# A hybrid-mixer trunk on one core: the GLA decay beside its values, the mLSTM weight products among the pairs

## Chip, core and metric

One of the eight cores of a Trainium2 chip runs the whole kernel. The metric is the device time of one execution in microseconds (us), taken as the median of several. The core has a matrix engine (PE, TensorE), a vector engine (DVE), a scalar engine (ACT), GpSimd (POOL), SyncE (SP, which here only issues transfers) and 16 DMA engines.

## What is computed

For 2048 tokens of width 1024 the reference computes one layer: RMSNorm, a combined input projection, four causal token mixers in parallel (a gated linear recurrence RG-LRU, an mLSTM with matrix memory, an HGRN2 recurrence and a gated linear attention, GLA), a projection of each mixer's output, a merge by sigmoid gates, an output projection, the residual and a final RMSNorm. All is float32.

```python
u = jnp.einsum('bsd,de->bse', h, w_in).astype(jnp.float32)
...
q = headwise(xm, m_wq)
k = headwise(xm, m_wk)
v = headwise(m_x, m_wv)
qkv = jnp.concatenate([q, k, v], axis=-1)
log_i = qkv @ m_wi + m_bi
log_f = jax.nn.log_sigmoid(qkv @ m_wf + m_bf)
...
log_gk = jax.nn.log_sigmoid(g_lr @ g_w_lr2 + g_b_lr2) / GLA_GATE_TAU
og = gla_chunkwise(split_heads(g_q, GLA_HEADS), split_heads(g_k, GLA_HEADS),
                   split_heads(g_v, GLA_HEADS), split_heads(log_gk, GLA_HEADS))
...
proj = jnp.einsum('bsnw,nwd->bsnd', branches, w_branch)
gates = jax.nn.sigmoid(merge.reshape(B, S, N_BRANCH, D_MODEL))
merged = jnp.sum(gates * proj, axis=2)
return merged @ w_out
```

The change touches the two places where small weights meet: the products of mLSTM's q, k and v weights with each other and with the gate weights (they need no token), and GLA's decay `log_gk`, a product of rank 16.

## The kernel before

The tokens go through in two halves of 1024. Products are in float32 split into a high and a low part (tiles hh and hl of the activations, wh and wl of the weights), three matmuls for each. Each half has these stages, with the times of the first half:

- A prologue, 0 to about 100 us, once: `load_first` loads and scales tokens and computes the first gates (`proj_ch`, L268), `load_h` the other 512 tokens (L685 spreads the norm factors over the partitions with four small products into one bank, ACT copies them at L686, and eight L688 on DVE scale the tokens), `setup_mix` prepares constants, and `split_blocks` forms block sums (L375 to L378) and their splits (L305, L306).
- The pairs, to about 740 us: `ahead_pairs` computes two output tiles at a time by seven products of half size (`ip_pair`, L423, with sums L428 of weights and L432 of results on DVE). The order of the pairs and of the steps between them is the table GORD. Projected rows go to DRAM.
- The mixers, to about 1200 us: `mixers` runs twelve steps of HGRN and GLA tiles (`gla_tile`, L959 to L1107; its scans are L968 and L970, its last products L1102 and sums L1103), and the generator `mlstm` beside them. Direct projections fill PE meanwhile: `ip_vals` (L280, its results copied at L1123 and, for the 8 columns of the low-rank decay in each of two groups, to lrt at L1125) and the gates of `gates_ahead`.
- The merge, to about 1290 us: four branches, each with its input read back and split (`branch`, L1292 and L1293), then products L268 with the gate applied at L1319; and `outp`.

What sets the order on the engines is a scheduler that simulates a timeline; instructions are emitted under `prio` offsets (EV 6000 for loads and evacuations, MIX 4000 for mixers), and the scheduler takes ready ones by priority. Buffers then decide who waits: the arena is a list of slots of 516 columns, given out in turn (`T` one slot, `F` two), so whoever writes a slot waits for the last reader of its earlier contents. PSUM has eight banks: two of them (pb, by `pbank`) take the direct projections in turn, six (mx, by `bank`) the mixers and small products. In the pairs all eight go round.

`setup_rows` does not exist before. Its work stands in `setup_mix`, L612 to L634: five loads (mwv, three weights of 512 columns and m_wg of 96), two memsets, and for each of four heads four products (L623 of 128x128; L626, L627 and L631 of 8 columns) in three banks, with five DVE copies (L624 to mqk, L628 and L629 to gx, L632 and L633 to gv).

`gla_decay` turns lrt round (eight transposes L1168, two copies L1169 into the slot pair lt), multiplies it by wlr (four products L1175) and puts each through ACT (L1177 to L1179 and a logarithm) and DVE (L1181, L1182). The mixers call it ahead of step 7; its results are used from step 8 on, while `ip_vals(3)`, which completes lrt, is called ahead of step 6.

Of the kernel before, what the change touches and what calls it, by code (L numbers as in the profile page):

```python
# [38 lines left out]
SI = 6  # L39
RLAT = 2000  # L40
LAT = -600
GORD = [('g',2),('r',1),('z',1),('g',1),('z',1),('r',1),('g',1),('z',2),('r',1),('g',1),('z',2),('r',1),('z',6),('g',3),('t',0),('m',0),('g',1),('m',0),('g',1),('m',0),('g',1),('m',0),('d',0),('m',0),('g',99),('d',1),('z',2)]
NORM = {"hz": "hnw", "gz": "gnw"}
SILU = ("lz", "mz", "hq", "hz", "gz")
FILL = [0, 2, 0, 0, 0, 1, 0, 0, 1, 0, 0, 0, 2, 0]
# [102 lines left out]
class Trunk:  # L148
# [312 lines left out]
        fin(c)  # L461
        self.free(*c)

    def ahead_pairs(self):


        nc = self.nc
# [70 lines left out]
        first = True  # L538
        for n, i in GORD:
            if n == "t":  # L540
                self.exp_ln()
            elif n == "m":
                with self.prio(RLAT):
                    next(rows, None)
            if n in "tm":
                continue
            for tiles, fin in ({"g": g, "z": z, "r": r}[n][:i] if n != "d" else [decays([2 * i, 2 * i + 1])]):
                self.ip_pair(*tiles, fin, first)
                first = False
            if n != "d":  # L550
                del {"g": g, "z": z, "r": r}[n][:i]
# [39 lines left out]
    def setup_mix(self):  # L591
        nc, c, a, col = self.nc, self.const, self.a, self.col
        V, A = nc.vector, nc.scalar

        lam = self.pvt[:, PV["lam"][0]:PV["lam"][0] + 4]
        t = col(4)
        self.clru = col(4)
        A.activation(t, lam, AF.Abs)
        A.activation(t, t, AF.Exp, scale=-1.0)
        A.activation(t, t, AF.Ln, bias=1.0)  # L600
        V.tensor_scalar(self.clru, lam, -1.0, 0.0, op0=ALU.mult, op1=ALU.max)
        V.tensor_tensor(self.clru, self.clru, t, op=ALU.add)
        V.tensor_scalar(self.clru, self.clru, 4.0, None, op0=ALU.mult)
        self.nclru = col(4)
        V.tensor_scalar(self.nclru, self.clru, -1.0, None, op0=ALU.mult)
        self.hba, self.hbx = col(4), col(4)
        V.tensor_scalar(self.hba, self.pvt[:, PV["ba"][0]:PV["ba"][0] + 4], 0.5, None, op0=ALU.mult)
        V.tensor_scalar(self.hbx, self.pvt[:, PV["bx"][0]:PV["bx"][0] + 4], 0.5, None, op0=ALU.mult)

        o = PV["mcw"][0]  # L610
        V.tensor_scalar(self.hmc, self.pvt[:, o:o + 20], 0.5, None, op0=ALU.mult)
        nc.sync.dma_start(self.mwv, a["m_wv"])  # L612
        V.memset(self.gx, 0.0)
        V.memset(self.gv, 0.0)
        wt = [self.T() for _ in range(3)]
        for w, n in zip(wt, ("m_wqT", "m_wkT", "m_wvT")):
            nc.sync.dma_start(w[:, :512], a[n].rearrange("p h d -> p (h d)"))
        wg = self.T()
        nc.sync.dma_start(wg[:, :96], a["m_wg"])
        for h in range(4):  # L620
            ps = self.bank()
            wq, wk, wv = (w[:, h * 128:(h + 1) * 128] for w in wt)
            nc.tensor.matmul(ps[:, 0:128], wq, wk, start=True, stop=True)  # L623
            V.tensor_copy(self.mqk[:, h], ps[:, 0:128])  # L624
            ps = self.bank()
            nc.tensor.matmul(ps[:, 0:8], wq, wg[:, h * 8:h * 8 + 8], start=True, stop=False)  # L626
            nc.tensor.matmul(ps[:, 0:8], wk, wg[:, 32 + h * 8:40 + h * 8], start=False, stop=True)  # L627
            V.tensor_copy(self.gx[:, h, 0:4], ps[:, 0:4])  # L628
            V.tensor_copy(self.gx[:, h, 32:36], ps[:, 4:8])  # L629
            ps = self.bank()  # L630
            nc.tensor.matmul(ps[:, 0:8], wv, wg[:, 64 + h * 8:72 + h * 8], start=True, stop=True)  # L631
            V.tensor_copy(self.gv[:, h, 0:4], ps[:, 0:4])  # L632
            V.tensor_copy(self.gv[:, h, 32:36], ps[:, 4:8])  # L633
        self.free(*wt, wg)  # L634

        lbl = self.pvt[:, PV["lbl"][0]:PV["lbl"][0] + 4]
        e, r, self.l1, self.alb, z = col(4), col(4), col(4), col(4), col(4)
        V.tensor_tensor(e, lbl, lbl, op=ALU.subtract)
        A.activation(e, e, AF.Exp)
        V.reciprocal(r, e)  # L640
        V.tensor_tensor(e, e, r, op=ALU.mult)
        V.tensor_tensor(e, e, e, op=ALU.subtract)
        A.activation(self.l1, e, AF.Ln, scale=-1.0, bias=1.0)
        V.tensor_scalar(z, e, 0.0, -1e30, op0=ALU.is_le, op1=ALU.mult)
        V.tensor_scalar(r, e, 1e-37, None, op0=ALU.max)
        A.activation(self.alb, r, AF.Ln)
        V.tensor_tensor(self.alb, self.alb, z, op=ALU.add)
        self.nalb = col(4)
        V.tensor_scalar(self.nalb, self.alb, -1.0, None, op0=ALU.mult)

        nc.sync.dma_start(self.wlr, a["g_w_lr2"])


    def load_h(self, half, xs, ns=(0, 1)):
# [504 lines left out]
    def gla_decay(self):  # L1159

        nc = self.nc
        V, A, T = nc.vector, nc.scalar, nc.tensor
        gs = []
        lt = self.F()
        for n in range(2):
            ps = self.bank()
            for c in range(4):
                T.transpose(ps[0:16, c * 128:(c + 1) * 128], self.lrt[:, n * 4 + c, :], self.cs("id"))  # L1168
            V.tensor_copy(lt[0:16, n * 512:(n + 1) * 512], ps[0:16])  # L1169
        for p in range(2):  # L1170
            gs.append([self.T(0, NU + 2 * NA if p else None) for _ in range(2)])
            for n in range(2):
                g, t = gs[p][n], self.T()
                ps = self.bank()
                T.matmul(ps, self.wlr[:, p * 128:(p + 1) * 128], lt[0:16, n * 512:(n + 1) * 512], start=True, stop=True)  # L1175
                gg, tt = g[:, :512], t[:, :512]
                A.activation(gg, ps, AF.Identity, bias=self.pv("gb", p))  # L1177
                A.activation(tt, gg, AF.Abs)
                A.activation(tt, tt, AF.Exp, scale=-1.0)  # L1179
                self.ln(tt, tt, bias=1.0)  # L1180
                V.scalar_tensor_tensor(gg, gg, 0.0, tt, op0=ALU.min, op1=ALU.subtract)  # L1181
                V.tensor_scalar(gg, gg, 1.0 / 16, None, op0=ALU.mult)  # L1182
                self.free(t)
        self.free(lt)
        return gs


    def mixers(self):
# [35 lines left out]
        for s, (j, gi) in enumerate(steps):  # L1224
# [4 lines left out]
            elif s == 6:  # L1229
                self.ar.lim = low  # L1230
                gv += self.ip_vals(3, 264, self.lrt[:, :, 8:16])
                self.ar.lim = None
            elif s == 7:
                with mix():
                    gd = self.gla_decay()
            if s + 1 < len(steps):
                load(s + 1)
            self.gates_ahead(next(fill))
# [140 lines left out]
    def build(self):  # L1379
# [35 lines left out]
        for half in range(2):  # L1415
# [4 lines left out]
            with self.overlay(NA + NY, F32R, f"s{half}_") as st:  # L1420
# [2 lines left out]
                    for i in range(NE):  # L1423
                        self.gate(32 - NP + i, (0,))
                self.split_blocks(x, st)
                self.ahead_pairs()
            oa, ob = more(NA, f"ma{half}_"), more(NY, f"mb{half}_")
            self.restore_block()
            self.mixers()
# [119 lines left out]
```

## Time and profile before

| | us |
|---|---|
| median of the timed runs | 2731.97 (2730.16 to 2736.35) |
| profiled execution | 2737.6 |
| span of its trace | 2735.8 |
| PE busy | 2604.2 |
| DVE busy | 1739.0 |
| POOL busy | 1500.4 |
| ACT busy | 1296.8 |

The mean granted clock of PE over the span is 0.977 of full speed. Matmuls are pipelined: a row with a duration of 0.40 us can stand 0.23 us behind the one before it, so that busy time is that of the union. "<-" in a name reads output from inputs; buffer numbers are left out, so mx is any of the six banks, mb and ma are arena slots of the mixers' stage, as arena itself and xb are slots. A wait is listed with the engine, line and tile that ended it.

### The profile page before, as it was taken

To read this page: it belongs to the slowest core of one execution; us is meant where nothing else is said; L and a number is where in the kernel's file an instruction comes from. 1 tells how busy PE (TensorE), PEld (TensorE's weight loads), DVE (VectorE), ACT (ScalarE), POOL (GpSimd) and SP (SyncE) were. 2 spreads that over 40 slices of the span, in tenths; PEclk is the share of its full clock that TensorE was granted. 3 is DMA by queue.
4 is the path that set the end of the run, shared out by engine and by line. 5 is a ranking of instruction groups with operands and counts; after the bars stand their busy time and mean duration, and the time that the engine had idled before them with its cause. 6 is when DMAs were issued, how large, how long until landed. Compare 5 with 4: busy or idle time off the path is not lost. (4 is left out here: it accounts for less than half of the span.)

```text
span 2735.8 us, 45795 instructions
## 1 busy us (share of the span) xinstructions
PE 2604.2 (95%) x16800; PEld 2155.0 (79%) x16800; DVE 1739.0 (64%) x2907; ACT 1296.8 (47%) x2769; POOL 1500.4 (55%) x1273
## 2 busy tenths in 40 slices
PE   7999999999998898999999999999999999999999
PEld 5777878878788886778977777788787888776789
DVE  8787676447667778634376957754657667775332
ACT  5455444434444464452454454454345455644533
POOL 5566556444555555466475566554445555654753
PEclk9999999999999998999999999999999989999999
DMA  6233223443454336785442432243346433558721
GB/s 227 70 127 104 85 85 131 135 135 112 156 178 126 103 123 205 271 288 160 140 139 77 140 115 85 89 131 124 123 131 203 129 106 120 183 168 289 260 95 74
DMA packets 227073, 393.03 MB, mean 144 GB/s; under 512 B 20721, under 2 KB 78081, under 8 KB 226849
## 3 DMA queue, kind: packets, MB, share of 16 engines
q1 hardware_dynamic: 226848, 390.11, 43.2%
q8 instruction: 132, 2.16, 0.3%
q14 instruction: 93, 0.75, 0.1%
HBM read 270.42 MB, written 119.60 MB: 143 GB/s over the span
## 5 line engine op out<-in xcount | busy, mean ns | idle before, releaser
L418 POOL TENSOR_TENSOR wl<-wr,wh 128x512 fp32r<-128x512 f32 x264 | 370.2, 1407 | 300.5 <-ACT wh L417 292.2
L418 POOL TENSOR_TENSOR wl<-gth,wh 128x512 fp32r<-128x512 f32 x198 | 286.4, 1447 | 280.7 <-ACT wh L417 266.7
L423 PE MATMUL mx<-s,wh 128*128 128x512 f32 x1248 | 395.0, 396 | 5.5 <-DVE arena L432 2.4
L432 DVE TENSOR_TENSOR arena<-arena,mx 128x512 f32<-128x512 f32 x386 | 252.8, 681 | 184.4 <-PE mx L423 168.1
L250 POOL TENSOR_TENSOR wl<-wr,wh 128x512 fp32r<-128x512 f32 (+1 forms) x176 | 248.5, 1420 | 194.1 <-ACT wh L249 159.3
L423 PE MATMUL mx<-hh,wl 128*128 128x512 f32 x824 | 328.1, 398 | 9.4 <-POOL wl L418 9.4
L423 PE MATMUL mx<-hh,wh 128*128 128x512 f32 x824 | 326.8, 397 | 5.8 <-DVE mqk L624 3.6
L423 PE MATMUL mx<-hl,wh 128*128 128x512 f32 x824 | 327.5, 397 | 2.4 <-DVE hl L306 2.3
L268 PE MATMUL pb<-hh,wh 128*128 128x512 f32 x704 | 291.0, 415 | 11.4 <-DVE lw L1319 4.0
L268 PE MATMUL pb<-hl,wh 128*128 128x512 f32 x704 | 287.6, 409 | 3.2 <-DVE hl L1293 3.2
L268 PE MATMUL pb<-hh,wl 128*128 128x512 f32 x704 | 286.5, 407 | 0.0
L423 PEld LDWEIGHTS mx<-s,wh 128*128 128x128 f32 x1248 | 235.7, 189 | 62.7 <-DVE arena L432 2.8
L417 ACT ACTIVATE wh<-wr 128x512 fp32r<-128x512 f32 x264 | 164.2, 627 | 229.0 <-PE mx L423 142.6
L280 PE MATMUL pb<-wh,hh 128*128 128x256 f32 (+1 forms) x880 | 254.2, 290 | 3.6 <-DVE lrt L1125 2.3
L280 PE MATMUL pb<-wl,hh 128*128 128x256 f32 (+1 forms) x880 | 253.9, 289 | 1.7 <-POOL wl L250 1.7
L280 PE MATMUL pb<-wh,hl 128*128 128x256 f32 (+1 forms) x880 | 253.5, 288 | 0.0
L423 PE MATMUL mx<-s,wl 128*128 128x512 f32 x624 | 245.5, 397 | 0.0
L417 ACT ACTIVATE wh<-gth 128x512 fp32r<-128x512 f32 x198 | 124.3, 628 | 228.5 <-DVE gth L428 184.4
L423 PEld LDWEIGHTS mx<-hh,wl 128*128 128x128 f32 x824 | 155.8, 189 | 51.5 <-POOL wl L418 16.0
L423 PEld LDWEIGHTS mx<-hh,wh 128*128 128x128 f32 x824 | 156.4, 190 | 46.3 <-issue 7.0
L249 ACT ACTIVATE wh<-wr 128x512 fp32r<-128x512 f32 (+1 forms) x176 | 110.2, 629 | 165.0 <-PE pb L268 110.1
L423 PEld LDWEIGHTS mx<-hl,wh 128*128 128x128 f32 x824 | 155.9, 189 | 41.1 <-DVE hl L306 3.6
(614 smaller groups left out, 6081.8 us busy)
## 6 DMA issues: line engine op xcount, KB each, us to landing
wr<-in_wc_dram SPq DMA_DIRECT2D x246, 256.0 KB, 2.7
g<-arena SPq DMA_DIRECT2D x52, 512.0 KB, 3.4
gth<-in_wc_dram SPq DMA_DIRECT2D x66, 256.0 KB, 2.8
wr<-in_wb_dram SPq DMA_DIRECT2D x64, 256.0 KB, 3.3
hl<-y SPq DMA_DIRECT2D x32, 512.0 KB, 5.9
arena<-g SPq DMA_DIRECT2D x48, 256.0 KB, 4.5
arena<-in_xT_dram SPq DMA_DIRECT2D x32, 256.0 KB, 5.2
lw<-g SPq DMA_DIRECT2D x32, 256.0 KB, 3.6
```

Source lines behind the costliest of these rows:

```text
L249: nc.scalar.activation(hi, raw, AF.Copy)
L250: nc.gpsimd.tensor_tensor(lo, raw, hi, op=ALU.subtract)
L268: nc.tensor.matmul(ps, w[:, ws], h[:, ts], start=(k == 0 and i == 0), stop=(k == nk - 1 and i == 2))
L280: self.nc.tensor.matmul(v, h[:, cs], w[:, ws], start=(first and i == 0), stop=(last and i == 2))
L417: A.activation(hi, w, AF.Copy)
L418: G.tensor_tensor(lo, w, hi, op=ALU.subtract)
L423: nc.tensor.matmul(ps, wp[:, ws], xp, start=(k == 0 and i == 0), stop=(k == 3 and i == 2))
L432: V.tensor_tensor(o, x, y, op=ALU.add)
```

## The change

It has three parts. The lines that leave `setup_mix` become `setup_rows(temp)`, which `ahead_pairs` calls in the first half alone as a step 's' of GORD, behind six 'z' pairs and ahead of three 'g' pairs; its four temporary tiles come from the slots that the pairs use for temporaries. `gla_decay` is called ahead of step 6, straight behind `ip_vals(3)` and under the same slot limit. And its six banks come from `pbank`. Behind the moved lines, line numbers are 7 or 8 higher: L623, L626, L627 and L631 become L648, L651, L652 and L656; L685 and L688 become L693 and L696; L968 becomes L976; L1168, L1169, L1175 and L1177 become L1176, L1177, L1183 and L1185.

```diff
-GORD = [...,('r',1),('z',6),('g',3),('t',0),('m',0),...]
+GORD = [...,('r',1),('z',6),('s',0),('g',3),('t',0),('m',0),...]
...
-    def ahead_pairs(self):
+    def ahead_pairs(self, later):
...
                 self.exp_ln()
+            elif n == "s":
+                if not later:
+                    self.setup_rows(temp)
...
-            if n in "tm":
+            if n in "stm":
...
         V.tensor_scalar(self.hmc, self.pvt[:, o:o + 20], 0.5, None, op0=ALU.mult)
...
+    def setup_rows(self, temp):
...
         nc.sync.dma_start(self.mwv, a["m_wv"])
         V.memset(self.gx, 0.0)
         V.memset(self.gv, 0.0)
-        wt = [self.T() for _ in range(3)]
+        wt = [temp() for _ in range(3)]
         for w, n in zip(wt, ("m_wqT", "m_wkT", "m_wvT")):
             nc.sync.dma_start(w[:, :512], a[n].rearrange("p h d -> p (h d)"))
-        wg = self.T()
+        wg = temp()
         nc.sync.dma_start(wg[:, :96], a["m_wg"])
         for h in range(4):
             ps = self.bank()
...
         lt = self.F()
         for n in range(2):
-            ps = self.bank()
+            ps = self.pbank()
...
                 g, t = gs[p][n], self.T()
-                ps = self.bank()
+                ps = self.pbank()
...
             elif s == 6:
                 self.ar.lim = low
                 gv += self.ip_vals(3, 264, self.lrt[:, :, 8:16])
-                self.ar.lim = None
-            elif s == 7:
                 with mix():
                     gd = self.gla_decay()
+                self.ar.lim = None
...
-                self.ahead_pairs()
+                self.ahead_pairs(half)
```

On PE in the prologue, gate 4's products (L268 into pb, 24 of them, of which the first two and the last two stand here) have L685 (L693 after) ahead of them. This is one piece of the difference, before with -, after with +:

```order
-L685 MATMUL mx_101<-cst,rsx 128x128 x4
-L623 MATMUL mx_102<-xb_248,xb_247 128x128
-L626 MATMUL mx_103<-xb_249,xb_247 128x8
-L627 MATMUL mx_103<-xb_249,xb_248 128x8
+L693 MATMUL mx_101<-cst,rsx 128x128 x2
 L268 MATMUL pb_98<-hh_63,wh_84 128x512
 L268 MATMUL pb_98<-hl_71,wh_84 128x512
...
 L268 MATMUL pb_98<-hl_78,wh_85 128x512
 L268 MATMUL pb_98<-hh_70,wl_91 128x512
-L631 MATMUL mx_104<-xb_249,xb_248 128x8
...
+L693 MATMUL mx_101<-cst,rsx 128x128 x2
+L423 MATMUL mx_99<-hh_67,wh_87 128x512
```

The products of the heads are gone from here, and the last two of the four spreading products stand behind gate 4 instead of ahead of it.

On PE in the first half's mixers, before: the end of `ip_vals(3)` (L280) and what follows it. L268 are gates, L1079 and L1080 products of a tile step; the other seven of the eight transposes L1168 stand ahead of this piece or behind it.

```order
L280 MATMUL pb_97<-wh_86,hl_78 128x264
L1168 MATMUL mx_102<-cst,lrt 16x128
L268 MATMUL pb_98<-hh_63,wh_87 128x512
L268 MATMUL pb_98<-hl_71,wh_87 128x512
L268 MATMUL pb_98<-hh_63,wl_93 128x512
L1080 MATMUL mx_104<-mb_4_5090,mb_3_5089 128x128
...
L1080 MATMUL mx_104<-mb_4_5090,mb_3_5089 128x128
L268 MATMUL pb_98<-hh_64,wh_87 128x512
L1175 MATMUL mx_103<-mb_6_5092,wlr 128x512
L268 MATMUL pb_98<-hl_72,wh_87 128x512
```

After, at the same place:

```order
L280 MATMUL pb_97<-wh_86,hl_78 128x264
L1176 MATMUL pb_98<-cst,lrt 16x128 x4
L1176 MATMUL pb_97<-cst,lrt 16x128 x4
L1183 MATMUL pb_98<-arena,wlr 128x512
L1183 MATMUL pb_97<-arena,wlr 128x512
L1183 MATMUL pb_98<-arena,wlr 128x512
L1183 MATMUL pb_97<-arena,wlr 128x512
L268 MATMUL pb_98<-hh_63,wh_87 128x512
L268 MATMUL pb_98<-hl_71,wh_87 128x512
```

The whole of the decay's PE work now stands in one row on the two pb banks, with gates behind it.

On DVE at the same time, before: step 6's scan L968 and the copies of `ip_vals(3)` (L1123, and L1125 to lrt).

```order
L1040 COPY ma_1_5080<-mx_103 32x4x32 x2
L968 SCALAR_TENSOR_TENSOR mb_1_5087<-cst,arena 128x512
L860 COPY mdec_218<-arena 128x4
L922 SCALAR_TENSOR_TENSOR Cst_176<-Cst_177,mdec_216,mx_104 128x129 x2
L1123 COPY ma_3_5082<-pb_98 128x128
L1125 COPY lrt<-pb_98 128x8
L1123 COPY ma_3_5082<-pb_97 128x128
```

After, the end of those copies (L1131 and L1133 now), the decay's copies L1177 and the scan L976:

```order
L1131 COPY arena<-pb_98 128x128
L1133 COPY lrt<-pb_98 128x8
L1131 COPY arena<-pb_97 128x128
L1133 COPY lrt<-pb_97 128x8
L1177 COPY arena<-pb_98 16x512
L1177 COPY arena<-pb_97 16x512
L976 SCALAR_TENSOR_TENSOR arena<-cst,arena 128x512
L1189 SCALAR_TENSOR_TENSOR ma_0_5079<-ma_0_5079,mb_1_5087 128x512
```

The scan of step 6 moved from ahead of all these copies to behind all of them and behind the decay's own two; its target is now a slot of the arena that lt had.

## Rows read from the trace of the kernel before

**Rows 1.** The page's busy times: us, share of the span, instructions.
```profile
PE 2604.2 (95%) x16800; PEld 2155.0 (79%) x16800; DVE 1739.0 (64%) x2907; ACT 1296.8 (47%) x2769; POOL 1500.4 (55%) x1273
```

**Rows 2.** Windows: PE, PEld, DVE, ACT, POOL busy (instructions), clock, DMA share, GB/s.
```profile
40.00:60.00 20.00, 15.41 (x80) 13.09 (x78) 18.61 (x33) 8.02 (x13) 8.65 (x6) 0.83 0.38 132
60.00:80.00 20.00, 14.65 (x47) 10.88 (x48) 20.00 (x24) 8.15 (x14) 16.14 (x11) 0.77 0.12 41
...
450.00:500.00 50.00, 50.00 (x218) 40.55 (x217) 26.50 (x40) 24.30 (x40) 23.35 (x18) 1.00 0.32 107
```

**Rows 3.** Windows of the mixers in both halves.
```profile
953.00:985.00 32.00, 29.20 (x340) 27.95 (x340) 25.50 (x70) 13.58 (x43) 14.48 (x17) 1.00 0.29 84
985.00:1200.00 215.00, 199.52 (x1944) 154.62 (x1943) 138.14 (x255) 114.69 (x313) 106.73 (x107) 0.94 0.68 230
2302.00:2335.00 33.00, 30.67 (x362) 28.81 (x362) 26.82 (x72) 13.49 (x40) 15.70 (x18) 1.00 0.31 96
2335.00:2550.00 215.00, 200.66 (x1941) 155.05 (x1940) 136.78 (x255) 116.22 (x309) 108.99 (x106) 0.94 0.67 226
```

**Rows 4.** PE's waits in 0 to 130 us: what ended them, us, times, longest.
```profile
PE pb L423 <- DVE gv L633: 4.0, 1, 4.0
PE mx L423 <- DVE mqk L624: 3.6, 1, 3.6
```

**Rows 5.** PE's timeline in the prologue: start, us, line, tiles, [idle before].
```profile
47.99 0.47 PE L623 MATMUL mx<-xb,xb 128*128 128x128 f32 x2
...
48.88 0.47 PE L623 MATMUL mx<-xb,xb 128*128 128x128 f32 x2
...
63.00 0.77 PE L423 MATMUL mx<-hh,wh 128*128 128x512 f32 x1 [3.64 <-DVE mqk L624]
```

**Rows 6.** DVE's timeline in the prologue.
```profile
42.52 8.57 DVE L688 SCALAR_TENSOR_TENSOR arena<-arena,pvt,xb 128x512 f32<-128x512 f32 x8
...
52.82 0.68 DVE L353 TENSOR_TENSOR gth<-pb,xa 128x512 f32<-128x512 f32 x1
...
62.51 0.15 DVE L633 COPY gv<-mx 128x4 f32<-128x4 f32 x1
62.58 0.28 DVE L624 COPY mqk<-mx 128x128 f32<-128x128 f32 x1
...
91.03 1.99 DVE L432 TENSOR_TENSOR arena<-arena,mx 128x512 f32<-128x512 f32 x3
```

**Rows 7.** Lines of gla_decay, 975 to 1022: ns min/median/max, first and last start.
```profile
L1169 DVE COPY mb<-mx x2: 667/672/678, 982.7 to 999.4; 16x512 f32<-16x512 f32 x2
...
L1175 PE MATMUL mx<-mb,wlr x8: 587/588/692, 991.7 to 1005.6; 16*128 16x512 f32 x8
...
L1177 ACT ACTIVATE arena<-mx,pvt x3: 670/677/687, 1004.1 to 1006.5; 128x512 f32<-128x512 f32 x3
```

**Rows 8.** Step 6's and 7's scan, and the copies to lrt, first half.
```profile
L968 DVE TENSOR_TENSOR_SCAN mb<-cst,arena x2: 1225/1226/1226, 953.1 to 972.6; 128x512 f32<-128x512 f32 x2
...
L1125 DVE COPY lrt<-pb x8: 148/156/159, 955.1 to 990.3; 128x8 f32<-128x8 f32 x8
```

**Rows 9.** Last mixer sum L1103, last split L1293, last branch's start, both halves.
```profile
1199.32 0.69 DVE L1103 TENSOR_TENSOR arena<-mx,arena 128x512 f32<-128x512 f32 x1 [2.37 <-PE mx L1102]
...
1220.09 2.25 DVE L1293 TENSOR_TENSOR hl<-hl,hh 128x1024 fp32r<-128x1024 f32 x1
...
1241.38 0.40 PE L268 MATMUL pb<-hh,wl 128*128 128x512 f32 x1
1241.61 0.40 PE L268 MATMUL pb<-hh,wh 128*128 128x512 f32 x1
...
2551.92 0.69 DVE L1103 TENSOR_TENSOR arena<-mx,arena 128x512 f32<-128x512 f32 x1 [2.38 <-PE mx L1102]
...
2569.89 1.32 DVE L1293 TENSOR_TENSOR hl<-hl,hh 128x1024 fp32r<-128x1024 f32 x1
...
2594.17 0.39 PE L268 MATMUL pb<-hh,wh 128*128 128x512 f32 x1
```

More of the change, by code (lines that the diff above doesn't have):

```diff
@@ L41 @@
 LAT = -600
-GORD = [('g',2),('r',1),('z',1),('g',1),('z',1),('r',1),('g',1),('z',2),('r',1),('g',1),('z',2),('r',1),('z',6),('g',3),('t',0),('m',0),('g',1),('m',0),('g',1),('m',0),('g',1),('m',0),('d',0),('m',0),('g',99),('d',1),('z',2)]
+GORD = [('g',2),('r',1),('z',1),('g',1),('z',1),('r',1),('g',1),('z',2),('r',1),('g',1),('z',2),('r',1),('z',6),('s',0),('g',3),('t',0),('m',0),('g',1),('m',0),('g',1),('m',0),('g',1),('m',0),('d',0),('m',0),('g',99),('d',1),('z',2)]
 NORM = {"hz": "hnw", "gz": "gnw"}
@@ L611, in setup_mix @@
         V.tensor_scalar(self.hmc, self.pvt[:, o:o + 20], 0.5, None, op0=ALU.mult)
+        lbl = self.pvt[:, PV["lbl"][0]:PV["lbl"][0] + 4]
+        e, r, self.l1, self.alb, z = col(4), col(4), col(4), col(4), col(4)
+        V.tensor_tensor(e, lbl, lbl, op=ALU.subtract)
+        A.activation(e, e, AF.Exp)
+        V.reciprocal(r, e)
+        V.tensor_tensor(e, e, r, op=ALU.mult)
+        V.tensor_tensor(e, e, e, op=ALU.subtract)
+        A.activation(self.l1, e, AF.Ln, scale=-1.0, bias=1.0)
+        V.tensor_scalar(z, e, 0.0, -1e30, op0=ALU.is_le, op1=ALU.mult)
+        V.tensor_scalar(r, e, 1e-37, None, op0=ALU.max)
+        A.activation(self.alb, r, AF.Ln)
+        V.tensor_tensor(self.alb, self.alb, z, op=ALU.add)
+        self.nalb = col(4)
+        V.tensor_scalar(self.nalb, self.alb, -1.0, None, op0=ALU.mult)
+        nc.sync.dma_start(self.wlr, a["g_w_lr2"])
+    def setup_rows(self, temp):
+        nc, a = self.nc, self.a
+        V = nc.vector
         nc.sync.dma_start(self.mwv, a["m_wv"])
@@ L634, in setup_mix @@
         self.free(*wt, wg)
[L636 to L651, printed above, removed]
     def load_h(self, half, xs, ns=(0, 1)):
```

## The prediction

> **What bounds the kernel now.** I read the page's busy shares first: PE is busy 95% of the span, 2604.2 of 2735.8 us [rows 1], so whatever is won or lost is a stop of PE, a slower granted clock, or PE work that moves from under such a stop to where there is none. The reader is to see that the largest engine leaves only 131.6 us.
>
> Then the windows, stage by stage [rows 2]. In the prologue PE is busy 15.41 and 14.65 us of 20, at a granted clock of 0.83 and 0.77, while DVE is busy 18.61 and 20.00: DVE sets that stretch. In the pairs, 450 to 500 us, PE is busy 50.00 of 50 at clock 1.00 and DVE only 26.50: PE alone sets it, and any PE work put there lengthens the run by its own duration. The mixer's later part, 985 to 1200 and 2335 to 2550, has PE at 199.52 and 200.66 of 215 with the clock at 0.94 [rows 3]: about 15 us of stops and, by (1 - 0.94) x 200, some 12 us of slow clock in each half. That is where a better or worse order shows.
>
> Last, single rows: who ends PE's waits in the prologue [rows 4], and when the steps around the change begin and end [rows 5 to 9].
>
> **Part one, setup_rows out of the prologue.** What it removes there: per head four products, which on PE take 48.88 - 47.99 = 0.89 us from one head's L623 to the next [rows 5], so 3.6 us for four heads; five small DVE copies a head; four loads into arena slots and one into mwv; and two waits of PE, 4.0 us (put down to the gv copy L633) and 3.6 us for the mqk copy L624, before which PE stood idle until 63.00 [rows 4, 5].
>
> Do the 7.6 us of waits come back? Only if PE's next goal is not a DVE result. It is: the first pair's sums, L432, begin at 91.03 [rows 6], after a DVE chain without gaps, and every bank that PE fills before then is emptied by that chain. So the question is when the chain ends. Its first long piece, the eight L688 from 42.52, reads ACT's copy of a bank that L685 fills in four pieces. The order shows that the last two of these now come behind gate 4's 24 products: 24 x 0.23 = 5.6 us later (0.23 is what lies between two such products at full clock, as 1241.61 stands behind 1241.38 [rows 9]). Against this the chain loses the setup copies, 0.28 for mqk and four of 0.15 a head; as 62.51 and 62.58 stand 0.07 apart, they fill some 0.20 + 4 x 0.07 = 0.48 a head, 1.9 us in all. And it does two L428 and gate 4's L353, of one shape and 0.68 us each [rows 6], ahead of L688 in the hole. Sum: 5.6 - 1.9 - 3 x 0.68 = +1.7 us; as some products of pair one that were behind the release now come ahead of it, I take **+1 us**. Bounds: all of the 7.6 us won, -7.6, and the whole hole of 5.6 us kept.
>
> What it adds: the same PE work between two pairs at about 490 us, where PE has no stop: **+3.6 us**, nothing hides it. The lower end would be none of it (if PE did wait there in places), the upper 4.5 us with a wait of 0.9 us for an arena slot. The copies go to a DVE that is half idle there, and the SP queue carries five more loads among the pairs' own, at a DMA share of 0.32 [rows 2]: nothing for both, though a pair load caught behind a setup load that waits for its slot would stop PE, and that is what the upper bound has. Its results (mqk, gx, gv) are first needed by the row steps of the pairs, far behind.
>
> Part one: +1 + 3.6 = **about +4.6 us**, between -7.6 and +10.
>
> **Part two, gla_decay straight behind ip_vals(3).** Its instructions stay the same in number. On PE they now stand in a row: eight transposes and four products with nothing between, two banks in turn. PE must sit through the DVE copy (0.67 us, L1169) and, for the third and fourth product, through the ACT pass that empties the bank (0.68 us, L1177) [rows 7]. Each product is two passes of 0.59 us that overlap, near 0.9 us in all, so most of the ACT time is covered: I count 0.7 + 2 x 0.3, about 1.3 us a half, where before the other work between them left under 1 us. That is **+0.5 us a half**, at least 0, at most 0.67 + 2 x 0.68 = 2 us.
>
> The larger effect is on step 6. Before, its scan L968 ran at 953.1, ahead of ip_vals(3)'s copies L1125, which go from 955.1 to 990.3 [rows 8]. Now the scan's target is the arena slot that gla_decay's lt leaves free, so it waits for the last reading L1175, and DVE's order shows it behind both L1177 copies (L1169 of before). Step 6, step 7 and the mLSTM chunk beside them then begin some 30 us later. Meanwhile PE runs ip_vals(3) and gates without a mixer between: in 953 to 985 and 2302 to 2335 it lost 2.8 and 2.3 us [rows 3], and these I give back. But the mixer work of that stretch, 25.50 and 26.82 us of DVE, goes into the next 215 us, where DVE has 138.14 and 136.78 already [rows 3]: 163 of 215, room in the mean, but not for single chains.
>
> Is the end of the mixer late? Summing the rows of PE's order with the trace's durations puts the last L1102 12 us (second half 17 us) of PE work later than before. Before, its L1103 came at 1199.32, the last split of the branch that it feeds at 1220.09 + 2.25 = 1222.3, and the last branch's products began near 1241.6, so 19 us were to spare; in the second half 2551.92, 2571.2 and 2594.2, 23 us [rows 9]. 19 - 12 = 7 and 23 - 17 = 6 us remain: the merge is not stopped by it, if the steps keep up with PE's order. They have 215 us less 30 plus 12 to 17, about 200 us, for what took 215, plus gla_decay done. I expect more stops of PE inside, from rows with the same pace: 27 us of loss a half over 215 us is 0.126 us per us, and the 26 us of mixer work that come in addition bring 26 x 0.126 = 3.3 us. Less the 2.5 us given back: **+0.8 us a half**. Bounds: half of the 15 us of stops gone (-7), or PE stopped by the whole squeeze of 215 - 200 = 15 us less the 6 us of slack (+9).
>
> **Part three, pbank in place of bank.** Twelve banks fewer are asked of the mixer's six, twelve more of the projections' two. Nothing in the rows waits for a mixer's bank at that place; the cost is in part two. Zero.
>
> A rule speaks against parts two and three. The order leaves four groups on two banks, and the row says that a bank is held 0.68 us by ACT [rows 7]. The Trainium skill, page Perfetto Trace Analysis, section Optimizing Tensor Performance (Matmuls), says that independent groups should rotate through different banks so that emptying one overlaps the next. By it PE would lose the whole 2 us a half instead of 1.3, by the row's overlap little of that; no run here has yet shown the two-bank form.
>
> **Sum.** +1 + 3.6 + 2 x 0.5 + 2 x 0.8 = +7.2; as the terms for the prologue and the squeeze are the softest, and both have their far end on the winning side, I take **+6 us**. The profiled execution took 2737.6 us and would take 2743.6; it lies 5.6 us above the median of 2731.97, so the median becomes **2738 us**.
>
> **Rivals.**
> 1. *The mixer's instructions are ready when PE reaches them (faster).* Coming 12 to 45 us of PE work later in PE's order while their inputs from other engines are not all late, they stop PE less: if a third of the 27 us of loss a half goes, that is -9 each, -18 + 4.6 = -13: 2718; with a smaller share, 2725. It decides from -2.3 us a half on, where it pays for the setup's work. For it: the loss there is large and small stops are made of DVE and ACT results just missed. Against it: step 6 is late by a real dependence, and DVE, idle near 975, is fuller behind it.
> 2. *The squeeze bites (much slower).* The steps cannot make up the 30 us, the last branch is late by 6 to 9 us a half, and the splits of the merge fall on the same DVE: 2 x 9 + 4.6 = +22: 2754. For it: the step is bound by a chain of DVE, ACT, POOL and PE. Against it: 19 and 23 us to spare.
> 3. *Nothing is seen.* The prologue gives back as much as the pairs take, and the tail pays for itself: 2732. That the change does not do what it says belongs here: the mixers' banks are freed where none was waited for.
> 4. *The clock falls at gla_decay.* After PE's idle 3.64 us, its products took 0.77 us and the stretch ran at 0.77 of the clock [rows 2, 5]; between the levels of 2.4 and 1.2 GHz that is (1 - 0.77) x 20 = 4.6 us. Once a half more, +9 on top of +6: 2747. The pieces of idle time here are far shorter than 3.64 us, so I hold it unlikely. The Trainium skill, page TensorE: Matmul & The Clock Gate, section A second HAM failure mode: psum-queue depth-cycling, tells of short idles between groups, with banks used in turn, that cost a kernel its clock; by that rule it would happen here, and no row of before shows it for idles this short.
>
> **How the numbers follow.** Forecast (2733 to 2745) 0.37; rival 1 0.24; rival 2 0.11; rival 3 (2728 to 2733) 0.22; rival 4 0.06. A range from 2717 to 2756 leaves out the far part of rival 1, some 0.09, and of rival 2, some 0.05, and things not thought of. A difference below 0.2%, 5.5 us, is about what a measurement of this kernel cannot tell from none: faster means below 2726.5, slower above 2737.4. Faster: rival 1 but for its weak end, plus a little of rival 3, 0.24. Slower: rivals 2 and 4 and some 0.25 of the forecast's 0.37, 0.42. Same: 0.34.
>
> **What would show it.** Right: no L624 wait in the prologue, the first L432 within 3 us of 91; 3.6 us of L648 to L656 products near 490 us and everything behind them later by about 4 to 5; step 6's scan near 990 rather than 953; the last mixer product 5 to 15 us later, and no long PE wait at the last branch. Wrong: pairs that begin earlier than before by more than 3.6 us; a stretch 985 to 1215 with PE's loss below 20 us (rival 1), or PE waits over 5 us for the last branch's splits (rival 2).

## The result, and the profile after

The changed kernel takes 2813.5 us (2809.8 to 2816.2); the kernel before, on the same chip, 2734.16. The ratio is 1.029, 95% interval 1.027 to 1.031: 79 us slower, where 6 us slower was forecast and 2756 was the upper end. The profiled execution has a span of 2812.0 us, 76 us more than before.

The page of the changed kernel, part 1 (us, share, instructions), beside [rows 1]:

```profile
PE 2632.2 (94%) x16800; PEld 2172.5 (77%) x16800; DVE 1739.5 (62%) x2907; ACT 1305.3 (46%) x2775; POOL 1492.9 (53%) x1273
```

The work is the same; PE is busy 28 us longer, which is a slower clock, and idle 48 us longer. To find the place I gave each matmul of both traces its usual spacing at full clock, summed these in the order of each trace, and looked at where the real time runs away from that sum. At the start of the mixers the changed kernel is about 8 us behind. At the work that the kernel before reaches at 1170 us it is some 13 to 16 us behind, and at that of 1230 us 49 us. The second half begins 48 us late (its first scan at 2138.43 instead of 2090.00). There the delay first shrinks to some 32 to 36 us, at the work of 2520 us, and is 70 us at that of 2580 and 76 at the end. So most of it arises in two short stretches at the end of the mixers. Their windows in the changed kernel (stretch, PE, PEld, DVE, ACT, POOL busy, granted clock, DMA share, GB/s):

```profile
1200.00:1225.00 25.00, 16.00 (x261) 12.10 (x259) 14.23 (x29) 15.93 (x44) 9.32 (x12) 0.71 0.79 284
1225.00:1250.00 25.00, 19.31 (x96) 14.07 (x96) 6.11 (x13) 14.60 (x38) 15.14 (x14) 0.54 0.76 245
1250.00:1275.00 25.00, 23.11 (x92) 18.00 (x93) 9.77 (x13) 14.85 (x27) 19.22 (x15) 0.93 0.76 259
...
2575.00:2600.00 25.00, 13.28 (x119) 9.57 (x117) 11.28 (x19) 12.82 (x26) 11.73 (x11) 0.72 0.79 284
2600.00:2625.00 25.00, 22.45 (x196) 16.93 (x196) 8.07 (x17) 13.39 (x34) 14.03 (x13) 0.87 0.67 210
2625.00:2650.00 25.00, 17.12 (x67) 13.49 (x68) 8.23 (x10) 14.87 (x30) 17.97 (x13) 0.88 0.70 233
```

The same view of before, 75 us around its last mixer sums:

```profile
1165.00:1240.00 75.00, 71.86 (x402) 56.42 (x401) 26.94 (x38) 37.08 (x76) 52.48 (x40) 1.00 0.81 276
2520.00:2595.00 75.00, 74.41 (x412) 58.55 (x411) 25.88 (x39) 39.14 (x78) 53.91 (x42) 1.00 0.79 263
```

In each set of the changed kernel PE stands idle for 17 and 22 of 75 us, where it was 3 and 1, and by the clock column it loses another 15 us (0.29 x 16.0 + 0.46 x 19.3 + 0.07 x 23.1) and 9 us, where it lost nothing. That is some 59 of the 76 us. No other engine is full there. PE waits for one mixer step; what it waits for longest between 1200 and 1280 (us, times, longest):

```profile
PE mx L1001 <- ACT ma L1058: 5.2, 1, 5.2
PE mx L1044 <- DVE ma L1024: 4.2, 1, 4.2
```

These are products of one `gla_tile` step (L993 and L1036 of before), each for the ACT or DVE pass just ahead of it. In the second half the longest wait between 2575 and 2660 is again one of L1001, 9.7 us. The end of the mixers in DVE's timeline, beside [rows 9] (first half):

```profile
1249.93 0.68 DVE L1111 TENSOR_TENSOR arena<-mx,arena 128x512 f32<-128x512 f32 x1
...
1257.25 0.68 DVE L1111 TENSOR_TENSOR arena<-mx,arena 128x512 f32<-128x512 f32 x1
...
1271.89 1.22 DVE L1300 TENSOR_TENSOR hl<-hl,hh 128x1024 fp32r<-128x1024 f32 x1
```

And the first product of the last branch in PE's timeline, both halves. It is the 192nd product from the end of the merge, by the same count that gives 1241.61 and 2594.17 in [rows 9]:

```profile
1290.87 0.39 PE L268 MATMUL pb<-hh,wh 128*128 128x512 f32 x1
...
2664.60 0.39 PE L268 MATMUL pb<-hh,wh 128*128 128x512 f32 x1
```

The last mixer sum comes at 1257.25, 58 us later than before (1199.32). The last branch is not held up by its splits. It starts 17.8 us after the end of the last one (1273.1), where it had 19 us to spare, and 16.5 us after it in the second half (2648.1). What stops PE are the mixers' own products, which stand ahead of this in PE's order. How much of that order is left behind the last of them (L1102, and L1110 after) shows in windows of L268 alone, from that product on (stretch, PE busy with the number of products, clock, DMA share, GB/s); first the two halves of before, then those of the changed kernel:

```profile
1199.10:1310.00 110.90, 88.02 (x375) 1.00 0.63 213
2551.75:2700.00 148.25, 87.98 (x375) 1.00 0.39 129
```

```profile
1256.65:1356.00 99.35, 77.52 (x324) 0.98 0.53 175
2631.25:2760.00 128.75, 75.21 (x302) 0.96 0.37 119
```

The changed kernel has done 51 and 73 more of these products by then, at 0.23 us each 12 and 17 us of work. Of the 58 us by which the mixers end late, that leaves 58 - 12 = 46 us in the first half, and the second half does begin 48 us late. In the second half the last sum comes 80 us late, and 80 - 17 = 63 of the 76 us are there at the end of the mixers. The start of the delay in DVE's timeline, step 6's scan and step 7's:

```profile
992.29 1.23 DVE L976 TENSOR_TENSOR_SCAN arena<-cst,arena 128x512 f32<-128x512 f32 x1 [2.85 <-PE pb L1183]
...
1048.91 1.23 DVE L976 TENSOR_TENSOR_SCAN arena<-cst,mb 128x512 f32<-128x512 f32 x1 [1.94 <-DMA y<-arena]
```

The store of step 6's result that it waits for, in SP's timeline:

```profile
1043.99 0.38 SPq L1114 DMA_DIRECT2D y<-arena  x1
```

Step 6 begins at 992.29 instead of 953.1 [rows 8], when the decay's last product L1183 has read the slot; 8 of these 39 us are those of the pairs, 31 its own. That I had foreseen. Step 7's scan, which followed 20 us behind step 6's (972.6), now follows 57 us behind it: it waits for a store that step 6 sends off at its very end, since its slot held step 6's gates. That I had not looked for. Listing what the arena gives out, call by call, from the two kernels' code shows why: while step 6 is laid out, the decay's four results are held as well, 39 of the 40 slots are taken (35 at most before), and 11 of the 15 tiles of step 6 take a slot that gla_decay or step 6 itself has just left (6 of 15 before).

### The profile page after: what moved, and what is told of

It is laid out like the page before. It is cut to its first block, busy times and chain, and to the rows that moved or that the text cites. A ratio compares the mean times of both kernels' runs of the same rounds, so it can differ in the third digit from the quotient of the medians.

```text
span 2812.0 us, 45809 instructions
## 1 busy us (share of the span) xinstructions
PE 2632.2 (94%) x16800; PEld 2172.5 (77%) x16800; DVE 1739.5 (62%) x2907; ACT 1305.3 (46%) x2775; POOL 1492.9 (53%) x1273
## 5 line engine op out<-in xcount | busy, mean ns | idle before, releaser
L423 PE MATMUL mx<-s,wh 128*128 128x512 f32 x1248 | 396.9, 397 | 7.1 <-DVE s L306 3.1
L432 DVE TENSOR_TENSOR arena<-arena,mx 128x512 f32<-128x512 f32 x386 | 252.5, 680 | 186.1 <-PE mx L423 169.0
L423 PE MATMUL mx<-hh,wl 128*128 128x512 f32 x824 | 328.0, 398 | 9.4 <-POOL wl L418 9.4
L423 PE MATMUL mx<-hl,wh 128*128 128x512 f32 x824 | 327.5, 397 | 4.2 <-DVE hl L306 4.1
L423 PE MATMUL mx<-hh,wh 128*128 128x512 f32 x824 | 326.8, 397 | 3.0 <-ACT wh L417 3.0
L268 PE MATMUL pb<-hh,wh 128*128 128x512 f32 x704 | 296.8, 423 | 23.9 <-DVE arena L1326 9.1
L268 PE MATMUL pb<-hl,wh 128*128 128x512 f32 x704 | 291.8, 415 | 0.3 <-DVE hl L1300 0.3
L268 PE MATMUL pb<-hh,wl 128*128 128x512 f32 x704 | 290.1, 412 | 0.0
L423 PEld LDWEIGHTS mx<-s,wh 128*128 128x128 f32 x1248 | 237.0, 190 | 65.1 <-DVE s L306 4.9
L280 PE MATMUL pb<-wh,hh 128*128 128x256 f32 (+1 forms) x880 | 253.4, 289 | 4.1 <-DVE lrt L1133 3.3
L280 PE MATMUL pb<-wl,hh 128*128 128x256 f32 (+1 forms) x880 | 252.7, 288 | 0.9 <-POOL wl L250 0.9
L280 PE MATMUL pb<-wh,hl 128*128 128x256 f32 (+1 forms) x880 | 252.8, 288 | 0.3 <-DVE hl L1338 0.3
L423 PE MATMUL mx<-s,wl 128*128 128x512 f32 x624 | 246.3, 398 | 0.0
L423 PEld LDWEIGHTS mx<-hh,wl 128*128 128x128 f32 x824 | 155.6, 189 | 51.5 <-POOL wl L418 16.3
L423 PEld LDWEIGHTS mx<-hh,wh 128*128 128x128 f32 x824 | 156.4, 190 | 43.4 <-ACT wh L417 4.0
L423 PEld LDWEIGHTS mx<-hl,wh 128*128 128x128 f32 x824 | 156.0, 189 | 43.3 <-DVE hl L306 5.8
L268 PEld LDWEIGHTS pb<-hh,wh 128*128 128x128 f32 x704 | 140.1, 199 | 63.4 <-ACT arena L1316 5.6
```

The costliest lines, as they stand in the source:

```text
L268: nc.tensor.matmul(ps, w[:, ws], h[:, ts], start=(k == 0 and i == 0), stop=(k == nk - 1 and i == 2))
L280: self.nc.tensor.matmul(v, h[:, cs], w[:, ws], start=(first and i == 0), stop=(last and i == 2))
L423: nc.tensor.matmul(ps, wp[:, ws], xp, start=(k == 0 and i == 0), stop=(k == 3 and i == 2))
L432: V.tensor_tensor(o, x, y, op=ALU.add)
```

## Experiments

Each was timed beside the kernel before on its own chip; us are differences of the medians, with the 95% interval of the ratio. "Parts" are the change's three.

**The parts apart.** Part one alone, part two alone, part three alone, and two with three; each edit is that share of the change's diff.

> Part one alone: setup_rows in the pairs, gla_decay as before. Slot theory (the loss of the mixers comes from arena slots that gla_decay's earlier call holds and hands on): this part is only the 8 us by which the changed kernel's pairs end later, so +6 to +10 us on the kernel before. Rival (the pairs' new arena use shifts the slots of the mixers as well): +20 us or more.

Measured +8.9 us, 1.0031 (1.0019 to 1.0044).

> Parts two and three alone: gla_decay behind ip_vals(3), on the pb banks; setup_rows stays in the prologue. Slot theory: nearly all of the loss, +62 to +74 us. Rival (the parts act on each other): under +50 us.

Measured +75 us, 1.0269 (1.0248 to 1.0290).

> Part three alone: gla_decay ahead of step 7 as before, on the pb banks. Slot theory: banks do not matter, within 5 us of the kernel before. Rival (the two-bank form stops PE and the projections): +25 us or more.

Measured +17.5 us, 1.0056 (1.0026 to 1.0086): outside what either theory said.

> Part two alone: gla_decay behind ip_vals(3) on the mixers' banks. Slot theory: the loss stays, +50 to +75 us, since the arena slots are the same. Rival (banks): under +20 us.

Measured +70 us, 1.0254 (1.0228 to 1.0279).

So the parts nearly add up (9 + 75 = 84, for 79), the earlier call of gla_decay carries the loss, and the banks are worth 5 us on top of it. Alone, in the old place, the pb banks cost 17 us, and I have no mechanism for that: the PE waits of that trace are those of before within 3 us a line, and its steps 8 and 9 even end some 4 us sooner. The page tells only of what kind the loss is: PE is idle as long as before (2750.9 - 2618.3 = 132.6 us, for 131.6) and busy 14 us longer with the same 16800 instructions. Its six timed runs go with their mean granted clock, 2737.0 and 2740.6 us at 0.979 and 0.978, 2747 to 2754 at 0.972 to 0.974. Of the 15 us by which its trace is longer, 11 are there when the second half begins (2101.45 instead of 2090.00), and in this first half the clock around the decay itself is 1.00 (980 to 1020 us). So most of it is lost elsewhere, and why stays open.

**The late start alone.** The kernel before, with one copy that ties step 6 to the end of ip_vals(3):

```diff
         Gc, g8 = self.T(), self.T()
+        if self.wait:
+            V.tensor_copy(Gc[:, 0:16], self.lrt[:, 7, :])
...
             x, zs = loads.pop(s)
+            self.wait = s == 6
```

> The kernel before with one thing added: step 6's scan first copies 16 columns of lrt into its own slot, so that it cannot begin until ip_vals(3) has written its last columns (about 988 us). No decay is moved, no slot or bank changes hands. Late-start theory (what costs is that step 6 and all behind it begin some 30 us late, and that PE's other work runs out before the last step): +30 to +60 us. Rival (what costs is the fuller arena, or the decay's own work in that place): under +15 us.

Measured +33.7 us, 1.0122 (1.0100 to 1.0144). DVE's timeline shows the copy doing what it should:

```profile
984.21 0.15 DVE L1127 COPY lrt<-pb 128x8 f32<-128x8 f32 x1
984.40 0.39 DVE L969 COPY mb<-lrt 128x16 f32<-128x16 f32 x1
984.83 2.26 DVE L970 TENSOR_TENSOR_SCAN mb<-cst,arena 128x512 f32<-128x512 f32 x1
```

The window behind 1200 shows how PE falls idle at the end:

```profile
1200.00:1275.00 75.00, 65.99 (x370) 51.20 (x369) 24.52 (x36) 32.96 (x72) 51.89 (x42) 0.98 0.69 225
```

With step 6 begun 32 us late, the last mixer sum comes at 1234 instead of 1199: the 246 us from step 6's scan to the last sum did not shrink (249). PE had done 94 products L268 more by then, 22 us of work, so that 35 - 22 = 13 us remain; the second half begins 14 us late. A late start of step 6 in both halves, with nothing else changed in the program, costs 34 us together.

**No handed-on slots.** Parts two and three, with the decay's passing tiles elsewhere (and its four results still in the arena):

```diff
-        lt = self.F()
+        lt = self.lw.rearrange("p a b -> p (a b)")
...
-                g, t = gs[p][n], self.T()
+                g, t = gs[p][n], self.glt
...
-                self.free(t)
-        self.free(lt)
...
+        self.glt = c.tile([P, 512], F32, name="glt")
```

> Parts two and three, but gla_decay's lt lies in lw and its four passing tiles in one tile of their own, so that it hands no arena slot to step 6; its four results stay in the arena. Slot theory: step 6's scan runs at about 955 again, not at 985, and the loss falls to between +10 and +40 us, what is left being step 7, whose scan still takes a slot of step 6. Rival (gla_decay's early place on PE, DVE and ACT itself delays the steps): over +55.

Measured +34.6 us, 1.0117 (1.0096 to 1.0139), 40 us less than with the slots handed on. The scan's rows of this kernel (ns min/median/max, first and last start; step 6 at 951.6, step 7 at 968.7):

```profile
L968 DVE TENSOR_TENSOR_SCAN arena<-cst,mb x2: 1198/1208/1217, 924.1 to 968.7; 128x512 f32<-128x512 f32 x2
L968 DVE TENSOR_TENSOR_SCAN mb<-cst,arena x1: 1226/1226/1226, 951.6 to 951.6; 128x512 f32<-128x512 f32 x1
```

Both start as in before. Yet their sums come at 1014.7 and 1070.0, against 1001.0 and 1046.6, and the last one at 1227.9.

**Step 7 freed from step 6.** Parts two and three, with a rule for step 7 alone: of the free slots the one free longest, and none that step 6 keeps to its end.

```diff
+            if self.lru:
+                us.sort(key=lambda u: max(self.freed.get(i, 0) for i in range(u, u + k)))
...
+            self.ar.lru = s == 7
+            held = [u for u in self.late if not self.ar.used[u]] if s == 7 else []
+            for u in held:
+                self.ar.used[u] = True
```

> Parts two and three, but step 7 takes the arena slots that have been free longest, and none in which step 6 keeps its values, gates or last product; everything else as in parts two and three (+73.5 us). Slot theory: step 7's scan no longer waits for step 6's store; it begins within 25 us of step 6's scan instead of 56, and the loss falls to between +35 and +58 us. Rival (the steps are a chain of results whatever their slots): no change, +65 to +80.

Measured +67.4 us, 1.0252 (1.0232 to 1.0273). Both scans in DVE's timeline:

```profile
983.62 1.23 DVE L973 TENSOR_TENSOR_SCAN arena<-cst,arena 128x512 f32<-128x512 f32 x1 [3.27 <-PE pb L1183]
...
1026.29 1.22 DVE L973 TENSOR_TENSOR_SCAN mb<-cst,mb 128x512 f32<-128x512 f32 x1
```

A miss: step 7 no longer waits for the store, but it still comes 43 us behind step 6, and only 6 to 8 us are won. The visible wait of step 7 was not the second big term.

**Both at once, on either kind of bank.** The two edits together; and the same with `bank()` in gla_decay.

> Both: gla_decay's passing tiles off the arena, and steps 6 and 7 take the slots free longest, step 7 none that step 6 keeps to its end. Slot theory: nearly all of the loss is gone, -5 to +20 us. Rival (early place or chain): over +50.

Measured +23.7 us, 1.0081 (1.0059 to 1.0102).

> As own_and_free (+24 us), but gla_decay takes the mixers' banks again. If the two-bank form is what is left there (bank_only: +15 to +17 us), this comes to -5 to +12 us. If the early place of gla_decay itself or the four slots held two steps longer cost the rest, it stays at +18 to +30.

Measured +29.1 us, 1.0109 (1.0088 to 1.0129): the time does not fall with the mixers' banks, and some 24 to 29 us remain with step 6 early and the passing tiles gone. But the two kernels do not lose alike. With the pb banks PE is idle as long as before (131.5 us) and busy 14 us longer; with the mixers' banks it is idle 17 us longer and busy 11, and the last sum comes at 1230.4 instead of 1190.7. So this pair does not show what is left.

**The decay late, its passing tiles off the arena; and the same with its result slots taken early.** The first is decay_own's edit on the kernel before. The second adds to it:

```diff
                 gv += self.ip_vals(3, 264, self.lrt[:, :, 8:16])
+                self.gres = [[self.T(0, NU + 2 * NA if p else None) for _ in range(2)] for p in range(2)]
...
-            gs.append([self.T(0, NU + 2 * NA if p else None) for _ in range(2)])
+            gs.append(self.gres[p])
```

> The kernel before, with gla_decay in its old place and on the mixers' banks, but its passing tiles off the arena (lt in lw, one tile of its own). A try for a faster kernel: step 7 takes its slots from others than gla_decay's. Late-start theory: nothing waits there for those slots in the trace of before, so -5 to +5 us.

Measured +8.5 us, 1.0037 (1.0021 to 1.0053): no gain, and a little outside the range given. Step 7's scan comes 25 us late here (997.6).

> As late_own (+8.5 us: decay ahead of step 7, passing tiles off the arena), but its four result slots are taken ahead of step 6 already and lie unused till then. Theory of the full arena (39 of 40 slots taken in step 6, so that each of its tiles takes a slot just left): +25 to +45 us. Rival (the decay's work in its early place costs it): +3 to +14 us.

Measured +31.3 us, 1.0106 (1.0083 to 1.0128). Its two scans and the next, as rows of the line:

```profile
L968 DVE TENSOR_TENSOR_SCAN mb<-cst,arena x1: 1225/1225/1225, 948.8 to 948.8; 128x512 f32<-128x512 f32 x1
L968 DVE TENSOR_TENSOR_SCAN arena<-cst,mb x1: 1197/1197/1197, 965.9 to 965.9; 128x512 f32<-128x512 f32 x1
L968 DVE TENSOR_TENSOR_SCAN ma<-cst,arena x1: 1206/1206/1206, 1046.0 to 1046.0; 128x512 f32<-128x512 f32 x1
```

Here no work of the decay is early. Four slots that lie unused during steps 6 and 7 cost 31.3 - 8.5 = 23 us (15 to 30 by the two intervals), and the steps show the picture of decay_own: both begin in time, their sums come at 1010.5 and 1060.0, the last at 1226.1. That is the second term. How a full arena does it is argued, not shown: from step 6's seventh tile on, 7 of its 15 take a slot that the step itself has left, where in late_own it is 6, from the tenth on, and whoever takes such a slot waits for its last reader. No row here tells which of these waits makes the 23 us.

**Which slot is given out.** The longest-free rule (the first diff of step7_free, with `self.ar.lru = True` through all the steps) on parts two and three, and on the kernel before.

> Parts two and three (+73.5 us) with the slot that has been free longest given out through all the steps, as in slots_longest_free (-12.5 us on the kernel before). Step 6's first two tiles then take slots that others left long ago, but its next three still take those that gla_decay leaves, since no others are free. Theory (late start by handed-on slots, and the fuller arena): +25 to +55 us. Rival (order of the work, not slots): +60 to +75 us.

Measured +14.0 us, 1.0044 (1.0026 to 1.0061), where parts two and three cost 75: outside my range, on the better side.

```profile
935.71 1.30 DVE L973 TENSOR_TENSOR_SCAN mb<-cst,mb 128x512 f32<-128x512 f32 x1
...
1019.53 1.21 DVE L973 TENSOR_TENSOR_SCAN ma<-cst,mb 128x512 f32<-128x512 f32 x1
```

Step 6's scan (the first row) runs at 935.7, ahead of the decay, whose call is where the change puts it; the last sum comes at 1202.4. So most of the 75 us hang on which free slot the arena hands over, not on the order of the work. How many of them depends on the kernel below, which wins 12.5 us by the same rule without the change: with the rule on both sides the change costs 14.0 + 12.5 = 26.5 us, some 49 less than 75.

> The kernel before, but through all the mixers' steps the arena gives out the slot that has been free longest, not the next one round. A try for a faster kernel: if waits for slots hold up steps in the kernel before too, -5 to -25 us; if its round-robin already finds old slots, -5 to +5 us.

Measured -12.5 us, 0.9962 (0.9951 to 0.9972): 2718.7 us, faster than both kernels. Its page, part 1:

```profile
PE 2597.8 (95%) x16800; PEld 2146.8 (79%) x16800; DVE 1735.3 (64%) x2907; ACT 1297.5 (48%) x2769; POOL 1494.0 (55%) x1273
```

and the windows that answer to [rows 3]:

```profile
985.00:1200.00 215.00, 197.96 (x1908) 151.01 (x1907) 129.05 (x240) 111.73 (x289) 103.85 (x106) 0.94 0.68 229
2335.00:2550.00 215.00, 196.01 (x1896) 149.51 (x1895) 132.66 (x238) 115.78 (x283) 115.65 (x108) 0.95 0.70 245
```

The windows do not look much better than before. In the second half the last sum comes at 2516.2 instead of 2551.9, but 446 products L268 are left behind the last mixer product there, not 375, so that 71 x 0.23 = 16 of these 36 us are only order. By the page PE is idle 5 us less and busy 6 us less over the span.

**L685 ahead of gate 4 again.** Part one, with

```diff
-                nc.tensor.matmul(ps[:, c * 128:(c + 1) * 128], r, self.cs("id"), start=True, stop=True)
+                with self.prio(0 if half else self.EV):
+                    nc.tensor.matmul(ps[:, c * 128:(c + 1) * 128], r, self.cs("id"), start=True, stop=True)
```

> Part one alone (+8.5 us), with the priority of loads given to L685's four small products, so that all four stand ahead of gate 4 again. My prediction's account (the late half of L685 holds up DVE's chain; the setup products cost 3.6 us in the pairs): the scan of the prologue ends earlier and +2 to +5 us is left. Rival (the prologue's order does not matter, or it is lost elsewhere): +7 to +10.

Measured +9.5 us, 1.0025 (0.9992 to 1.0057): too wide to tell +2 from +9, and open. Its trace has L688's scaling at 44.21 instead of 48.59, and yet the first sum L432 at 93.04 instead of 93.19 in the changed kernel.

The kernels side by side (scans and last sums of the first half, us from the span's start):

| kernel | change | step 6's scan | step 7's scan | last mixer sum |
|---|---|---|---|---|
| before | | 953.1 | 972.6 | 1199.3 |
| the change | +79 | 992.3 | 1048.9 | 1257.3 |
| parts23 | +75 | 982.8 | 1038.7 | 1244.5 |
| early_only | +70 | 970.5 | 1052.8 | 1240.5 |
| step7_free | +67 | 983.6 | 1026.3 | 1222.5 |
| delay_only | +34 | 984.8 | 1000.1 | 1234.0 |
| decay_own | +35 | 951.6 | 968.7 | 1227.9 |
| reserve_own | +31 | 948.8 | 965.9 | 1226.1 |
| own_free_mx | +29 | 961.0 | 1019.3 | 1230.4 |
| own_and_free | +24 | 958.2 | 998.5 | 1190.7 |
| slots_old | +14 | 935.7 | 1019.5 | 1202.4 |
| late_own | +9 | 952.0 | 997.6 | 1200.5 |
| slots_longest_free | -13 | 947.8 | 969.4 | 1194.4 |

A last sum past about 1220 goes with 29 us or more. An early one is no guarantee: behind own_and_free's last mixer product 432 products L268 are left in the first half, not 375, which is 13 us of work that PE has still to do.

## Why the prediction was wrong, step by step

**What bounds the kernel.** Right as far as it went: PE sets the pairs, and the difference arose as stops and slow clock of PE in the mixers' end.

**Part one.** Forecast +4.6 us, measured +8.9. Both terms were too small, the first inside its bounds, the second over its upper one (4.5). In the prologue the first sum L432 comes at 93.19 instead of 91.03 [rows 6], +2.2 where I took +1; but PE's products behind it were worse placed, with a new wait of 6.9 us (from PE's waits, 0 to 130 us), and the pairs run 3 to 5 us late ahead of the setup (this kernel and part1; kernels with the old prologue lie between -0.7 and +2.5 us there):

```profile
PE pb L423 <- ACT wh L417: 6.9, 1, 6.9
```

So the 7.6 us of waits [rows 4] did not come back, as I said, and others took their place. The setup in the pairs costs 5.2 instead of 3.6 us: by the products L423 this kernel is 3.3 us behind before it and 8.5 after it, part1 4.6 and 9.8. Part one alone shows why, in the window of the setup:

```profile
500.00:525.00 25.00, 25.00 (x119) 20.81 (x118) 11.31 (x33) 9.49 (x15) 9.46 (x8) 0.93 0.50 161
```

and in the products of 8 columns that the setup has there (row of the line):

```profile
L651 PE MATMUL mx<-arena x8: 172/256/256, 516.1 to 518.2; 128*128 128x8 f32 x8
```

The granted clock is 0.93 in that window and 1.00 in those on either side: (1 - 0.93) x 25 = 1.8 us that I had not counted.

**Part two.** This step failed. The late start of step 6 was read rightly (30 us; measured 31, and 39 with the pairs' 8), and the shift in PE's order too (12 and 17 us; measured 12 and 17). The 19 us of slack were a true figure, with 17.8 of them left after the change, but they were not the limit: PE stops ahead of the last branch, at products of the mixers. Wrong was the condition "if the steps keep up with PE's order", and the sentence that they "have 215 us less 30 plus 12 to 17, about 200 us, for what took 215" and would do it at 0.8 us a half. I took the steps' pace for PE's, to be had again by putting them closer. They did not keep up: from step 6's scan to the last sum it is 246 us before, 249 in delay_only and 265 in the changed kernel, and in the second half 250, 245 and 252. So the whole delay came to the end of the mixers, and what PE had not done ahead of it was lost: 58 - 12 = 46 us in the first half, 8 of them from part one. The bound of +9 a half rested on the same mistake. That the steps could not be faster is not shown: with other slots the same stretch takes 233 us in own_and_free and 277 in reserve_own (first half). Rival 2 had the mechanism ("The steps cannot make up the 30 us"), but looked for the cost at the last branch's splits, for which no long wait came, and used the same price list.

What I did not see at all was the second term. I followed one slot, the one that step 6's scan takes, and not how many were left: 39 of 40. That the four results are held two steps longer costs 23 us by reserve_own. With the late start (34 us by delay_only, 40 by decay_own) this makes 57 to 63 of the 75, if the two simply add, which no run shows; the rest, some 12 to 18, I cannot assign. PE's order may have a part in it: delay_only does 22 us of other products more ahead of the last mixer product in each half, the changed kernel 12 and 17.

**Part three.** Forecast nothing, measured 5 us with the rest of the change and 17 alone. The stall itself was small: for the decay's products PE waits 0.4 us twice, not the 1.3 us that I had counted. By the rule of the Trainium skill (page Perfetto Trace Analysis, section Optimizing Tensor Performance, Matmuls) that independent groups should rotate through different banks I had put it at up to 2 us; the 0.8 us of the trace are less than half of that. The clock was not small. Windows around the decay, changed kernel (first three rows), and early_only, where the same products go to the six banks with gates between (last two):

```profile
975.00:985.00 10.00, 10.00 (x86) 10.00 (x85) 1.20 (x7) 1.43 (x4) 1.04 (x1) 1.00 0.15 54
985.00:995.00 10.00, 9.22 (x37) 4.71 (x36) 3.59 (x7) 7.41 (x14) 6.26 (x7) 0.84 0.38 105
995.00:1005.00 10.00, 10.00 (x51) 7.77 (x50) 9.33 (x12) 7.78 (x15) 6.64 (x6) 0.82 0.25 78
```

```profile
970.00:980.00 10.00, 10.00 (x88) 9.11 (x87) 7.06 (x14) 7.36 (x15) 4.48 (x5) 1.00 0.05 11
980.00:990.00 10.00, 10.00 (x44) 7.65 (x43) 0.68 (x1) 3.02 (x5) 6.11 (x5) 1.00 0.58 174
```

Behind the row of transposes and 16-row products the clock falls to 0.84 and 0.82, and costs 0.16 x 9.2 + 0.18 x 10 = 3.3 us; in the second half it is 0.80 and 0.86 at the same place, 3.2 us. That is my rival 4, held unlikely at 0.06, and its 4.6 us a half was near. Not all of it need be the change's: in the kernel before the clock is 0.83 from 1005 to 1015 us, behind its own last decay product at 1005.6. The section of the Trainium skill that I set beside it (TensorE: Matmul & The Clock Gate, A second HAM failure mode: psum-queue depth-cycling) speaks of short idles between groups with banks used in turn. The trace agrees in that the clock falls with only 0.8 us of idle in all, but it cannot tell the idles from the narrow products as the cause.

**The other rivals.** Rival 1 (the mixers' products are ready when PE reaches them) did happen for a while: in the second half the delay shrank from 48 to some 32 to 36 us while PE ran ahead with other work. That work was then missing as cover for the late steps. Rival 3 did not happen.

## What to carry to other kernels

When one step of a chain is made to wait, first measure the chain's own length in the trace, from that step to its last product, and count the other work that stands behind that product in the busiest engine's order. If the chain gets no shorter, its whole delay arrives there, less the work that the engine does ahead of it in the meantime (58 - 12 and 80 - 17 us here). Slack at a later point does not help, and other work that runs ahead is cover spent, not time won. When a buffer's life begins earlier, count how many slots are left at that point and who left them last; a wait on a recycled slot is a dependence that no dataflow shows. And before moving work to relieve a ring of buffers, try which free one is handed out: the one free longest made this kernel 12.5 us faster with no instruction moved by hand.

## What the runs showed of the hardware

Two spots of narrow products in an otherwise full PE were followed by a slower granted clock, with little or no idle time: 0.93 over the 25 us window with the setup's products of 8 columns, and 0.80 to 0.86 in the 20 us from the decay's 16-row products on (both halves), where early_only, with gates between them, shows 1.00. What in these spots lowers the clock, no run shows. I had priced such products by their time on PE alone.
